# A two-branch sparse-attention decoder step: the prompt's compression units put into the first pair's products, and the samples' rows of W_out computed in column-tiled fp32 sets

## The chip, the cores and the metric

The kernel runs on one core of one Trainium2 chip, with one launch. The metric is device time in microseconds (us); the time before is the median of three runs. A profile of one execution comes beside it: what each engine did and when. The engines are PE (TensorE; PEld is its loading of weights, which overlaps the products), DVE (VectorE), ACT (ScalarE), POOL (GpSimd) and SP (SyncE, which here issues nearly all transfers). Lines such as L351 are lines of the kernel.

## The reference

One layer of a decoder, run for a prompt (512 tokens) and for 8 samples with one new token each and 1,024 cached tokens. Both share all weights. Cut to what matters here:

```python
shift, scale, gate = jnp.split(jax.nn.silu(c) @ w_ada + b_ada, 3, axis=-1)
h = x * (1.0 + scale[:, None, :]) + shift[:, None, :]
parts = jnp.split(h @ w_in, np.cumsum(IN_WIDTHS)[:-1], axis=-1)
...
def compress(kseq, pos_emb, w1, b1, w2, b2):      # blocks of 32 tokens, one every 16
    blk = kseq[:, idx] + pos_emb[None, None, :, None, :]
    blk = blk.transpose(0, 1, 3, 2, 4).reshape(bsz, n, g, CMP_LEN * dh)
    return jax.nn.gelu(blk @ w1 + b1) @ w2 + b2
...
y_a = (o_a * jax.nn.silu(a_z)) @ w_up_a
y_b = (o_b * jax.nn.silu(b_z)) @ w_up_b
mixed = (jax.nn.sigmoid(m_a) * y_a + jax.nn.sigmoid(m_b) * y_b) @ w_out
x_new = layer_norm(DEEPNORM_ALPHA * x + gate[:, None, :] * mixed, ln_g, ln_b)
```

`o_a` is native sparse attention (a compressed branch, a selected branch and a window), `o_b` is block-sparse attention. `compress` runs over the prompt's new keys and values, and over the cached ones of each sample. D_MODEL is 1,024, a head has 64 channels, and the compressed branch has two key/value heads.

## The kernel before

Activations lie transposed: channels on the 128 partitions, the 512 prompt tokens and 8 sample tokens along the free axis (NT = 520, worked in halves of HB = 260). Products of the heavy kind are made in three passes of a reduced fp32 format: a high part and the rest of each operand, as high x high, rest x high, high x rest. Splitting an operand costs an ACT cast (the high part) and a subtraction on DVE or POOL (`lo`, L362, recorded as L367). Which of the two subtracts is set by `LO_ENG`, three short patterns for three stages, cycled through.

*Order of the work.* Python generators with costs (`Flow`, `merge`) interleave several strands of work as they are written down. The order in which each engine then executes is written out by hand: `QUEUES` holds, for each of five engines, a list of numbers of its instructions, and `line_up` ties each to the one before it. `SLOTS` names, for each tile that rotates among buffers, which buffer each request takes.

*Start.* `ada` (L567) makes the adaLN vectors of 128 channels as fp32 products whose four members of a set write to 32 partitions each, on 32 columns of the array; `ada_h` (L575) makes the hidden tile h with its high part and rest; `early_mm` multiplies it with the weights of `kc`, `vc` and `ks` as soon as one tile of h is there. SP loads `cT`, the first constants and `bT` with three transfers (L640 to L643); x comes in eight rows (`load_x`, L544), four in tiles of the key/value pool and four in tiles of their own.

*Dense products.* `dense` (L690) makes 128 output channels in 48 products of 260 columns. Its weights come through a `Feed` (L408): a ring of four raw tiles of 128 x 1,024 (tag `wr`), each freed once its two halves are split into `hl`.

*Compression.* `units` (L926) takes 48 products: two (keys, values) times eight chunks of 256 channels times three passes. `phi_prompt` (L968) runs it for the prompt: 64 unit columns and 2 columns of position embedding, so products of 66 columns; from the last two columns comes the constant `cc`. Then `phi_pair` (L1013) runs it four times, each for a pair of samples, with 256 columns. `gelu` follows, and a second, small product (`second`). Both use the tile `u`, of which there are two buffers, one each for keys and values. The strand `phis` (L1145) runs beside the first dense products.

*The end.* `up` (L1631) makes the merged branch `m` for 128 channels, split; its 8 sample columns are copied, high part and rest, into `msh` (128 x 8 x 16). The output projection works in two halves of 512 output channels. The first half, `out_first` (L1800), goes along with `up`; the weights of the second half are loaded, split and kept by `load_second` (L1813) at the turns named in `SECOND`, and used at the end. Per tile of 128 prompt tokens `out_mm` takes 3 products for each of 8 channel tiles. The samples have products of their own, `out_samples` (L1708): for each of 8 channel tiles two products of 512 columns with 16 stationary columns, for both halves 32 in all. `samples` (L1713) adds their two parts with a small product (constant `selw`) and finishes their rows; `residual` and `norm` finish the prompt's.

Of the kernel before, what the change touches and what calls it, by code (L numbers as in the profile page):

```python
# [50 lines left out]
SECOND = [3, 4, 6, 7]  # L51
# [6 lines left out]
COPY_ENG = "daa"  # L58
NRAW, NHL, CRAW = 4, 3, 3
LO_ENG = "dp", "pd", "dp"  # L60
# [11 lines left out]
for _name, _w in (("ident", 128), ("seli", 10), ("rowmask", 1), ("ones", 1), ("p16", 1),  # L72
                  ("gsum", 128), ("oneb", 8), ("onem", 8), ("seln", 32), ("selx", 32),
                  ("selm", 4), ("w14", 14), ("w4", 4), ("maskn", 384), ("maskh", 128), ("maskm", 512),
                  ("selp", 128), ("sels", 32), ("selw", 32), ("selm4", 32)):
    _C[_name] = (_n, _n + _w)
    _n += _w
# [10 lines left out]
    "phi.u": "01010010101010",  # L88
    "ring.wr": "0133212023011031201301023120203102130321030123331202130231132102313021302",
    "kv.v2": "010101010",  # L90
    "kv.ev": "010101010101010011001100110011010101",
    "kv.kd": "012021021012012",
    "kv.kl": "01",
    "start.xr": "0123",
    "ps.s": "0101010101011010101010110100101101101011010010101001100010110011001101010101100110011001001110101100110101010101010101011001",
    "start.a": "01010101",
    "ps.d": "01210201201112002012102010202102120120110210210221012021021002201201200120201210210110210102120120012102102102101202102120220212102120221011"
        "20210",
    "ring.whl": "012012021021020120210120120120120120102102101202102012102102101202102101201201201020120120102012012012021210120",
    "phi.craw": "13200130120321302031",  # L100
# [3 lines left out]
    "at.q2": "0120120120120120",  # L104
    "at.qx": "0120120102102102",
    "at.mg": "01010101010101",
    "at.sm": "012345670123456701234567012354670123546701235467012354670123546701235467012354670123546701235467",
    "at.p3": "010101010101010101010101",
    "de.cr": "01200120120120120120120121202012012012012012",
# [12 lines left out]
    "fin.hs": "01",  # L122
# [6 lines left out]
0-1 5-8 2-3 20-23 9-12 24-27 4 13-17 34-35 18-19 36-41 31-33 28-30 42-55 58-63 56-57 67-69 95-97 64-66 92-94 70-77 89-91 81-83 123-125 86-88 84-85  # L129
78-80 120-122 98-105 109-111 151-153 114-116 106-108 148-150 112-113 126-133 117-119 140-141 145-147 176-178 137-139 142-144 134-136 162-164 154-161  # L130
170-172 165-169 179-181 207-209 182-189 204-206 222-224 196-197 193-195 173-175 201-203 198-200 190-192 210-212 225-227 231-233 219-221 213-215
228-230 216-218 246-251 234-239 252-257 240-245 258-263 270-275 264-269 276-281 310-312 282-285 313-318 335-338 319-321 286-289 322-324 290-297
325-330 342-344 298-301 345-356 302-305 357-359 306-309 360-362 390 363-365 339-341 331-334 366-389 415-419 403-408 391-396 409-414 397-402 420-425
444-447 432-437 467-475 426-431 476-481 491-493 482-484 438-443 494-496 515-520 466 497-505 485-490 506-508 454-459 509-511 521-526 448-453 460-465
527-538 512-514 539-544 551-562 545-550 563-574 587-592 602-616 575-586 632-634 656-673 617-622 635-637 623-628 638-643 629-631 644-655 680-685
674-679 692-697 686-691 698-703 749-757 704-709 716-721 758-760 710-715 761-763 593-595 764-766 773-775 596-598 776-781 722-733 767-769 782-784
797-802 770-772 599-601 785-787 734-739 803-808 821-826 788-793 827-832 794-796 833-844 857-862 809-820 863-868 845-856 869-880 890-907 914-916
908-910 917-922 911-913 740-742 926-931 923-925 950-955 932-934 944-949 935-937 743-748 962-967 938-943 956-961 968-979 1007-1012 986-991 980-985
1013-1018 992-997 881-889 1019-1042 1055-1060 1043-1048 998-1006 1049-1054 1097-1104 1061-1066 1079-1090 1129 1091-1096 1067-1072 1142 1105-1116
1167-1170 1073-1078 1117-1128 1136-1141 1183 1130-1135 1143-1154 1161-1166 1171-1176 1155-1160 1177-1182 1196 1184-1195 1203-1208 1215-1220 1197-1202  # L140
1282-1283 1209-1214 1268-1269 1231-1236 1227-1230 1221-1226 1237-1242 1244-1249 1298-1300 1243 1250-1255 1290-1291 1301-1305 1270-1275 1256-1267
1276-1281 1284-1289 1312-1313 1328-1329 1306-1311 1320-1321 1292-1297 1336-1339 1314-1319 1322-1327 1364-1365 1348-1351 1340-1345 1330-1335 1358-1359
1366-1373 1346-1347 1374-1375 1352-1357 1376-1395 1402-1407 1396-1399 1412-1417 1400-1401 1408-1411 1442-1447 1418-1421 1360-1363 1428-1431 1452-1459
1432-1433 1422-1427 1440-1441 1448-1451 1460-1467 1434-1439 1472-1479 1468-1471 1490-1495 1506-1507 1480-1485 1488-1489 1486-1487 1508-1513 1518-1523
# [199 lines left out]
def build(tc, A):  # L344
# [11 lines left out]
    def ld(out, x):  # L356
        return nc.sync.dma_start(out, x)  # L357

    D = {}
    turns, engs = [0], [LO_ENG[0]]  # L360

    def lo(out, x, hi, eng=None):  # L362

# [8 lines left out]
    with ExitStack() as es:  # L372
# [1487 lines left out]
        for k in range(8):  # L1860
            out_samples(p, k, keep[k])
# [134 lines left out]
```

## Time and profile before

| | us |
|---|---|
| median of 3 runs | 602.77 |
| the runs | 602.71, 602.77, 605.0 |
| the profiled execution | 605.51 |
| its span, first to last instruction | 603.8 |

The page has these parts: 1, busy time, share and instructions of each engine; 2, the span in 40 slices of about 15 us, with the clock that TensorE was granted (PEclk) and the DMA's load; 3, DMA queues; 4, the chain of work that ended last, by engine and by line; 5, the costliest groups of instructions, as line, engine, operation, out<-in, shapes, count | busy us, mean ns of one | idle us of the engine just before them, and what ended it; 6, DMA issues. Views that ask the trace further: groups that keep shapes apart, windows (busy time of each engine in a stretch), the timeline, the chain in order of time, and waits. Each timeline row has a start, a length, the engine, the line, out<-in, the shape, and in brackets the idle time before it. A product's recorded length overlaps with those of its neighbours.

### The profile page before, as it was taken

The numbers are of one execution on the slowest core, as the hardware profiler recorded it, in microseconds if no ns is written. First come the engines' busy times: TensorE is split into PE (matmuls) and PEld (weight loads), VectorE is DVE, ScalarE is ACT, GpSimd is POOL, SyncE is SP. The second block draws the span as 40 slices with busy tenths as digits, with TensorE's granted clock in tenths as the row PEclk, the third lists the DMA queues.
The fourth block names the chain that finished last, engine by engine and source line by source line (L and its number), as shares of the span: only waits on it lengthen the run. The fifth ranks groups of instructions, "written<-read, shape, count | busy, mean of one in ns | idle before, by whom it ended". The sixth has DMA issues, their size and how long they took to land.

```text
span 603.8 us, 13227 instructions
## 1 busy us (share of the span) xinstructions
PE 588.1 (97%) x4721; PEld 504.0 (83%) x4721; DVE 293.2 (49%) x824; ACT 291.3 (48%) x688; POOL 271.5 (45%) x317
## 2 busy tenths in 40 slices
PE   7999999999999999999999999999999999999994
PEld 4789999999997888878768899987878697989773
DVE  1556534334374664644363545676421245334187
ACT  2457565635546546634446454575534134233343
POOL 0222567563433724351446728346361455354406
PEclk9998899999999999999999999999999999999998
DMA  8995465811665574466968635822997996332403
GB/s 300 401 362 169 111 195 162 277 36 36 185 183 166 186 246 144 161 234 240 370 226 324 246 122 197 279 104 57 325 399 245 374 347 222 106 117 89 188 1 141
DMA packets 63955, 124.82 MB, mean 207 GB/s; under 512 B 8402, under 2 KB 26258, under 8 KB 63378
## 3 DMA queue, kind: packets, MB, share of 16 engines
q1 hardware_dynamic: 62482, 119.79, 58.6%
q0 software_dynamic: 1408, 4.20, 1.8%
q8 instruction: 37, 0.61, 0.4%
q14 instruction: 28, 0.23, 0.1%
HBM read 114.37 MB, written 9.58 MB: 205 GB/s over the span
## 4 chain that ended last, share of the span: by engine, by line
PE 79%; DVE 6%; DMA 5%; ACT 3%; POOL 2%; issue 2%; SPq 2%; POOLq 0%; ACTq 0%; DVEq 0%
PE d L351 47%; PE s L351 12%; PE e L351 7%; PE o L351 5%; PE pt L354 5%; PE pt L351 2%; SPq L357 2%; DMA raw<-w_cols 2%; DMA u<-ada_ss 1%; DMA raw<-ada_g 1%; DVE bn L1762 1%; DMA raw<-mobv 1%; POOL p L1243 1%; DVE xt L1758 1%; POOL u L367 1%
## 5 line engine op out<-in xcount | busy, mean ns | idle before, releaser
L351 PE MATMUL d<-hTh,hl 128*128 128x260 f32 (+1 forms) x1392 | 266.4, 288 | 0.7 <-POOL hl L367 0.5
L351 PEld LDWEIGHTS d<-hTh,hl 128*128 128x128 f32 (+1 forms) x1392 | 217.1, 189 | 5.0 <-issue 1.7
L351 PE MATMUL d<-hTl,hl 128*128 128x260 f32 (+1 forms) x704 | 199.7, 284 | 0.0
L351 PEld LDWEIGHTS d<-hTl,hl 128*128 128x128 f32 (+1 forms) x704 | 132.5, 188 | 0.0
L367 POOL TENSOR_TENSOR hl<-raw,hl 128x512 fp32r<-128x512 f32 x57 | 77.3, 1356 | 113.8 <-ACT hl L447 91.4
L447 ACT CAST hl<-raw 128x512 fp32r<-128x512 f32 (+1 forms) x111 | 68.0, 617 | 51.4 <-PE d L351 43.9
L1241 ACT ACTIVATE p<-s,sm 128x256 f32<-128x256 f32 (+3 forms) x96 | 50.6, 529 | 71.5 <-DVE sm L1238 47.7
L1243 POOL TENSOR_SCALAR p<-p,sm,gp 128x512 f32<-128x512 f32 (+3 forms) x64 | 42.4, 670 | 70.8 <-DVE sm L1242 57.9
L367 DVE TENSOR_TENSOR hl<-raw,hl 128x512 fp32r<-128x512 f32 (+1 forms) x54 | 43.0, 800 | 40.8 <-ACT hl L447 37.8
L351 PE MATMUL d<-yh,hl 128*128 128x260 f32 x256 | 47.2, 285 | 0.0
L351 PEld LDWEIGHTS d<-yh,hl 128*128 128x128 f32 x256 | 39.9, 188 | 3.1 <-issue 1.7
L354 PE MATMUL pt<-cst,p 128*128 128x128 f32 x240 | 39.9, 279 | 0.6 <-POOL p L1243 0.6
L1243 POOL TENSOR_SCALAR p<-p,sm,cst 128x128 f32<-128x128 f32 (+3 forms) x32 | 20.9, 661 | 38.6 <-ACT pp L1251 16.4
L354 PEld LDWEIGHTS pt<-cst,p 128*128 128x128 f32 x240 | 27.2, 141 | 12.8 <-POOL p L1243 3.0
L351 PE MATMUL d<-yl,hl 128*128 128x260 f32 x128 | 36.3, 283 | 0.0
L1251 ACT COPY pp<-pt 128x512 f32<-128x512 f32 (+1 forms) x48 | 22.9, 478 | 27.0 <-PE pt L354 26.4
L351 PE MATMUL s<-u,w1h 128*128 128x256 f32 (+1 forms) x160 | 35.0, 287 | 0.6 <-POOL u L367 0.3
L1236 DVE TENSOR_REDUCE sm<-s 128x1 f32<-128x128 f32 (+1 forms) x48 | 16.8, 354 | 37.1 <-PE s L351 30.7
L1238 DVE CUSTOM_DVE_ANT_0 s<-s,band 128x256 f32<-128x256 f32 (+1 forms) x48 | 17.3, 365 | 34.5 <-PE s L351 24.7
L351 PE MATMUL s<-kd,q 128*128 128x256 f32 (+3 forms) x96 | 33.0, 348 | 0.2 <-ACT p L1241 0.2
L351 PE MATMUL s<-kd,qx 128*128 128x256 f32 (+3 forms) x96 | 30.6, 322 | 0.0
L351 PEld LDWEIGHTS s<-u,w1h 128*128 128x128 f32 x160 | 28.2, 198 | 1.2 <-POOL u L367 0.5
(413 smaller groups left out, 1044.8 us busy)
## 6 DMA issues: line engine op xcount, KB each, us to landing
raw<-w_cols SPq DMA_DIRECT2D x46, 512.0 KB, 6.0
raw<-mobk SPq DMA_DIRECT2D x64, 256.0 KB, 4.5
raw<-mobv SPq DMA_DIRECT2D x64, 256.0 KB, 5.3
craw<-cmp SPq DMA_DIRECT2D x64, 128.0 KB, 2.8
u<-ada_ss SPq DMA_DIRECT2D x12, 512.0 KB
raw<-slck SPq DMA_DIRECT2D x64, 64.0 KB, 3.0
raw<-ada_g SPq DMA_DIRECT2D x8, 512.0 KB, 5.5
raw<-w_up SPq DMA_DIRECT2D x8, 512.0 KB
```

Source lines behind the costliest of these rows:

```text
L351: return mmraw(out, lhsT, rhs, start=start, stop=stop, skip_group_check=True)
L354: return nc.tensor.transpose(out, x, unit)
L357: return nc.sync.dma_start(out, x)
L367: (nc.gpsimd if eng == "p" else nc.vector).tensor_sub(out, x, f32(hi))
L447: nc.scalar.copy(h, src)
L1236: nc.vector.tensor_reduce(sm[:, 0:1], s[:, :b], axis=AX, op=OP.min)
L1238: nc.vector.tensor_tensor_reduce(out=s[:, b:n], in0=s[:, b:n], in1=j.band[:, 256 - (n - b):], scale=1.0, scalar=top, op0=OP.add, op1=OP.mi ...
L1241: nc.scalar.activation(pr, s[:, :n], AF.Exp, scale=-1.0, bias=sm[:, 1:2], accum_out=sm[:, 2:3])
L1243: D.setdefault("pool", []).append(nc.gpsimd.tensor_scalar(pr, pr, sm[:, 3:4], j.gate(i), op0=OP.mult, op1=OP.mult))
L1251: j.copied[gi] = (nc.scalar.copy if COPY_ENG[gi] == "a" else nc.vector.tensor_copy)(t[:, :n], p[:, :n])
L1758: nc.vector.tensor_add(xt[tt][:, c], xt[tt][:, c], p)
L1762: nc.vector.bn_stats(BN[tt][0][:, BN[tt][1]], xt[tt][:, c0 + k:c0 + min(k + 256, n)])
```

## The change

It does the following.

- The prompt's compression units join those of the first pair: `phi_pair(0)` gets `u` tiles of 16 x 161 x 2 columns (`PAIR` = 128 + 32 + 1; the last column of each half holds the position embedding), so its 48 products have 322 columns; the prompt's own 48 products of 66 columns, its own `gelu` and three products of its `second` are gone.
- `msh` holds the samples' columns of `m` in fp32, 128 x 8 x 32 with 24 zero columns. `out_samples` is called eight times (once in each `out_first`, once in each `load_second`) and makes four fp32 products of 256 columns from the raw weight tile of W_out, each on its own 32 columns of the array. They all add up in one PSUM tile. `selw` grows to pick rows out of four groups.
- `cT`, `bT` and the first constants are one tile and one transfer; x rows 4 to 7 use the tiles of rows 0 to 3; the first tile of h is made in two halves.
- `LO_ENG` gives way to two written lists, `HL_LO` (weights) and `LO` (the rest), with one letter for each subtraction.
- `SECOND` is [3, 5, 7, 8] in place of [3, 4, 6, 7], with the fourth load behind `out_first(6)`.
- `SLOTS` and all five lists of `QUEUES` are made anew.

```diff
-SECOND = [3, 4, 6, 7]
+SECOND = [3, 5, 7, 8]
...
+PAIR = 128 + 32 + 1
 NRAW, NHL, CRAW = 4, 3, 3
-LO_ENG = "dp", "pd", "dp"
+HL_LO = "dpdpdpdppdppdpddpdppdpdpdpdppdpdpdpdpdpdpdpdpdpdpdpdpdpdpdpdpdpdpdpdpdpdpdpdpdpdppddpdpdpdppdppddpdppddpdppddpd"
+LO = "dpdpdppdpdddppddppdddpddppdpddpddppddppdppddpdpdpdpdpdpdpddpdpdppddppddp"
...
-        def u_tile(dtype=F32R):
-            return pp.tile([128, 2, 2048], dtype, name="u", tag="u", bufs=2)
+        def u_tile(dtype=F32R, n=2048):
+            return pp.tile([128, 2, 16 * PAIR], dtype, name="u", tag="u", bufs=2)[:, :, :n]
...
-            D["act"] = nc.scalar.activation(hTh[:, j, :T], x[:, :T], AF.Identity, scale=s1[:, 0:1], bias=sh[:, 0:1])
+            if j:
+                D["act"] = nc.scalar.activation(hTh[:, j, :T], x[:, :T], AF.Identity, scale=s1[:, 0:1], bias=sh[:, 0:1])
+            else:
+                c = slice(0, HB)
+                nc.scalar.activation(hTh[:, j, c], x[:, c], AF.Identity, scale=s1[:, 0:1], bias=sh[:, 0:1])
+                nc.vector.tensor_scalar(h[:, c], x[:, c], s1[:, 0:1], sh[:, 0:1], op0=OP.mult, op1=OP.add)
+                nc.vector.tensor_sub(hTl[:, j, c], h[:, c], f32(hTh[:, j, c]))
+                c = slice(HB, T)
+                nc.scalar.activation(hTh[:, j, c], x[:, c], AF.Identity, scale=s1[:, 0:1], bias=sh[:, 0:1])
...
-        nc.sync.dma_start(cT, A["cT"])
+        nc.sync.dma_start(first_in, A["first"])
         load_ada(0)
-        nc.sync.dma_start(cst0, A["cst"][:, :NC0])
-        nc.sync.dma_start(bT, A["bT"])
...
-            us = [u_tile().rearrange("p x (k q u) -> p x q k u", k=16, q=16) for _ in range(2)]
+            n = 16 * (PAIR if bp == 0 else 128)
+            uv = [u_tile(n=n) for _ in range(2)]
+            us = [u.rearrange("p x (k c) -> p x k c", k=16)[:, :, :, :128].rearrange("p x k (q u) -> p x q k u", q=16) for u in uv]
+            if bp == 0:
+                yield from phi_prompt(*kcvc, uv)
...
-            nc.gpsimd.tensor_copy(msh[:, c, 0:8], f32(m[:, 0, T:]))
-            nc.gpsimd.tensor_copy(msh[:, c, 8:16], f32(m[:, 1, T:]))
+            nc.gpsimd.tensor_copy(msh[:, c, :NS], us[0][:, T:])
...
-        def out_samples(p, k, hl):
-            for x in range(2):
-                mm(p[:16], msh[:, k], hl[:, x], k == 0 and x == 0, k == 7 and x == 1)
+        def out_samples(half, i, raw):
+            c = half * 256
+            for k in range(2):
+                for x in range(2):
+                    mm(first[4][grp(2 * k + x), c:c + 256], msh[:, 2 * i + k], raw[:, k * 512 + x * 256:k * 512 + x * 256 + 256], i == 0 and half == 0, i == 3)
...
-                out_samples(first[4], i, hl)
+            out_samples(0, k // 2, W.raw[W.units[W.used][0]])
...
                 nc.scalar.copy(t[:, 0], src)
                 lo(t[:, 1], src, t[:, 0])
+            out_samples(1, i, raw)
...
         out_first(6)
-        halves = [fin.tile([16, 512], F32, name="hs", bufs=2) for _ in range(2)]
-        nc.scalar.copy(halves[0], first[4][:16])
+        load_second(3)
+        hs = fin.tile([128, 512], F32, name="hs")
+        nc.scalar.copy(hs, first[4])
...
-        p = p_d()
-        for k in range(8):
-            out_samples(p, k, keep[k])
-        nc.scalar.copy(halves[1], p[:16])
-        few = samples(halves)
+        few = samples(hs)
```

The parts of PE's new order that the prediction speaks of (numbers are places in the order in which the program is written; 3724 to 3731, 3852 to 3859, 3980 to 3987 and 4012 to 4019 are the samples' products):

```diff
+3694-3699 3682-3687 3709-3711 3706-3708 3728-3731 3705 3732-3737 3700-3702 3718-3720 3712-3714 3738-3749 3715-3717 3721-3723 3750-3755 3768-3773
...
+3756-3767 3774-3779 3852-3859 3780-3785 3792-3797 3834-3836 3786-3791 3798-3803 3828-3830 3804-3809 3837-3839 3831-3833 3849-3851 3840-3842 3816-3821
...
+3914-3919 3938-3943 3920-3925 4024-4026 3926-3931 4052-4054 3944-3955 3974-3976 3959-3961 3968-3970 3977-3987 4012-4019 4027-4029 4055-4060 3988-3990
```

More of the change, by code (lines that the diff above doesn't have):

```diff
@@ L133 @@
[L133 to L136, printed above, removed]
@@ L359, in build @@
     D = {}
-    turns, engs = [0], [LO_ENG[0]]
+    engs, hl_engs = iter(LO), iter(HL_LO)
     def lo(out, x, hi, eng=None):
         if eng is None:
-            eng = engs[0][turns[0] % len(engs[0])]
-            turns[0] += 1
+            eng = next(engs)
         (nc.gpsimd if eng == "p" else nc.vector).tensor_sub(out, x, f32(hi))
@@ L447, in split_to @@
                     nc.scalar.copy(h, src)
-                    lo(l, src, h)
+                    lo(l, src, h, next(hl_engs))
                     self.part[self.ns] = hl
@@ L589, in ada_h @@
             nc.vector.tensor_copy(hTh[:, j, T:], h[:, T:])
-            nc.vector.tensor_scalar(h[:, :T], x[:, :T], s1[:, 0:1], sh[:, 0:1], op0=OP.mult, op1=OP.add)
-            D["dve"] = nc.vector.tensor_sub(hTl[:, j], h, f32(hTh[:, j]))
+            c = slice(0 if j else HB, T)
+            nc.vector.tensor_scalar(h[:, c], x[:, c], s1[:, 0:1], sh[:, 0:1], op0=OP.mult, op1=OP.add)
+            c = slice(c.start, NT)
+            nc.vector.tensor_sub(hTl[:, j, c], h[:, c], f32(hTh[:, j, c]))
         def less_last(t, src, last):
@@ L947, in gelu @@
         def gelu(us, n):
-            bs = pp.tile([128, 257], F32, name="bsh")
+            bs = pp.tile([128, 2 * PAIR + 1], F32, name="bsh")
             nc.gpsimd.memset(bs[:, n:n + 1], 0.0)
@@ L982, in phi_prompt, with second_prompt @@
                         for l2 in range(2):
[L983 removed]
+                            cp(ut[OWN[l2], x, :, g, 128:160], v[OWN[g], :, :, l2])
             yield 3000
[L985 to L1000 removed]
+        def second_prompt(p, x2):
+            lo(ck2[:, 1, :], x2, ck2[:, 0, :], "d")
+            for g in range(2):
+                rows = slice(g * 32, g * 32 + 32)
+                nc.vector.scalar_tensor_tensor(cv2[rows, g], p[rows, 448:512], 0.5, b2v[rows], op0=OP.mult, op1=OP.add)
         craw, nraw = {}, [0]
@@ L1024, in phi_pair @@
                 yield 2600
-            before()
+            if before:
+                before()
             yield 300
-            uv = [u.rearrange("p x q k u -> p x (k q u)") for u in us]
-            gl = yield from units(256, lambda kv, x, l: uv[kv][:, x, l * 256:l * 256 + 256])
+            n //= 8
+            gl = yield from units(n, lambda kv, x, l: uv[kv][:, x, l * n:l * n + n])
+            width = 320 if bp == 0 else 256
             def second():
@@ L1145, in phis @@
         def phis():
-            second = yield from phi_prompt(*kcvc)
+            second = None
             for bp in range(4):
@@ L1619, in build @@
         yh, yl = [Y2[k][0] for k in range(8)], [Y2[k][1] for k in range(8)]
-        msh = fin.tile([128, 8, 16], F32R, name="msh")
-        nc.gpsimd.memset(f32(msh), 0.0)
+        msh = fin.tile([128, 8, 32], F32, name="msh")
+        nc.gpsimd.memset(msh, 0.0)
         cst3 = fin.tile([128, NC4 - NC3], F32, name="cst3")
```

311 lines of the change are left out of this document (151 added, 160 removed).

## The prediction

> **What bounds the kernel now.** I read the page first, its busy shares, its slices and its chain.
>
> ```profile
> span 603.8 us, 13227 instructions
> PE 588.1 (97%) x4721; PEld 504.0 (83%) x4721; DVE 293.2 (49%) x824; ACT 291.3 (48%) x688; POOL 271.5 (45%) x317
> PEclk9998899999999999999999999999999999999998
> PE 79%; DVE 6%; DMA 5%; ACT 3%; POOL 2%; issue 2%; SPq 2%; POOLq 0%; ACTq 0%; DVEq 0%
> ```
>
> PE has work in 97% of the span and no other engine in half of it, and the chain that ended last lies on PE for 79%. So a product taken away is worth its place in PE's queue, its pitch (the time from one product's end to the next one's), not its duration, because products overlap. From the chain and the timeline of PE, 260 and 256 columns first, then two forms that the change touches:
>
> ```profile
> 43.72 6.13 PE d L351 x51
> 94.32 2.88 PE s L351 x24
> 51.59 0.28 PE L351 MATMUL s<-u,w1h 128*128 128x66 f32 x1
> 51.70 0.28 PE L351 MATMUL s<-u,w1l 128*128 128x66 f32 x1
> 51.81 0.28 PE L351 MATMUL s<-u,w1h 128*128 128x66 f32 x1
> 572.99 1.55 PE L351 MATMUL e<-hl,msh 128*16 128x512 f32 x6
> L351 PE MATMUL e<-hl,msh 128*16 128x512 f32 x16 | 4.7, 395 | 0.4 <-DVE hl L367 0.4
> ```
>
> 51 products in 6.13 us and 24 in 2.88 us are 0.120 us each. A product of 66 columns follows the one before by 0.11 us: it saves nearly nothing by being a quarter as wide. For 512 columns, (1.55 - 0.395) / 5 = 0.231 us. Between 260 and 512 columns a column costs (231 - 120) / 252 = 0.44 ns.
>
> The slices show two eights in PEclk, so I cut the windows view there. Columns: window, its length, busy time of PE, PEld, DVE, ACT and POOL, granted clock, DMA share, GB/s.
>
> ```profile
> 50.00:56.80 6.80, 6.53 (x58) 6.42 (x58) 4.70 (x10) 6.31 (x12) 1.88 (x2) 1.00 0.61 186
> 56.80:63.60 6.80, 6.80 (x36) 6.80 (x36) 2.08 (x7) 1.91 (x5) 0.00 (x0) 0.50 0.20 60
> 63.60:70.00 6.40, 6.40 (x55) 6.17 (x55) 3.97 (x10) 5.18 (x13) 3.90 (x4) 1.00 0.20 63
> 59.87 0.40 PE L351 MATMUL s<-u,w1h 128*128 128x66 f32 x1
> 60.08 0.40 PE L351 MATMUL s<-u,w1l 128*128 128x66 f32 x1
> ```
>
> For 6.8 us the clock is halved: 36 products where the next 6.4 us hold 55, and 66 columns at a pitch of 0.21 us. That loses 6.8 / 2 = 3.4 us. It comes right after the stretch in which the 66-column products stand close together, the thinnest work between the head and the tail. The Trainium skill, in "TensorE: Matmul & The Clock Gate", section "What's actually happening", says that the array's clock is halved after a window of about 3.4 us of low activity and given back by activity; the clock of 0.50 behind the thin stretch agrees, though no run yet shows the cause.
>
> **The change part by part.** *Compression.* What goes are these products, and what stays wider is the third group:
>
> ```profile
> L351 PE MATMUL s<-u,w1h 128*128 128x66 f32 x32 | 7.7, 292 | 0.3 <-ACT u L983 0.3
> L351 PE MATMUL s<-u,w1l 128*128 128x66 f32 x16 | 4.9, 308 | 0.0
> L351 PE MATMUL s<-u,w1h 128*128 128x256 f32 x128 | 27.3, 286 | 0.4 <-POOL u L367 0.3
> 107.32 0.28 PE L351 MATMUL pt<-w2l,gl 128*128 128x64 f32 x1
> 107.43 0.28 PE L351 MATMUL pt<-w2h,gl 128*128 128x64 f32 x1
> ```
>
> 48 products at 0.11 us go: 5.3 us. The first pair's 48 grow from 256 to 322 columns: 48 x 66 x 0.44 ns = 1.4 us more. In the second product three of 64 columns go (3 x 0.11 = 0.3 us), three grow by 64 columns (0.1 us). Net -4.1 us at full clock. The prompt's own gelu chain goes too, and the copies of its units stay; both lie on ACT, DVE and POOL, about half idle. The first pair's products now wait for the prompt's copies and the cache chunks; before, the chunks' copies waited for the prompt's products, 4.29 us:
>
> ```profile
> 60.73 0.62 ACT L1022 CAST u<-craw 128x512 fp32r<-128x512 f32 x1 [4.29 <-PE s L351]
> ```
>
> That wait goes, and dense products (5.8 us for 48) have to fill PE meanwhile. I put this at nothing; without that cover it costs up to the same 4.3 us.
>
> *The clock.* With the 66-column products gone, the stretch of 50 to 57 us fills with products of 260 columns, as around it. I take -3.4 us, ends 0 and -3.4.
>
> *Samples.* 32 products of 512 columns at 0.231 us go: 7.4 us. In their place stand 32 fp32 products of 256 columns, in eight sets of four, each member on 32 columns of the array. The nearest row is the adaLN product, of the same form and width, 8 products recorded twice each, two sets:
>
> ```profile
> 17.30 0.28 PE L351 MATMUL d<-hTl,v 128*128 128x260 f32 x1
> 17.51 1.07 PE L351 MATMUL s<-u,cs 128*32 128x256 f32 x16
> 18.51 0.30 PEld L351 LDWEIGHTS d<-hTh,v 128*128 128x128 f32 x2 [0.41 <-issue]
> 18.51 0.51 PE L351 MATMUL d<-hTh,v 128*128 128x260 f32 x2
> ```
>
> The product before ends at 17.58 us and the sets at 18.58: 0.50 us a set. The next two products end 0.44 us later in place of 2 x 0.12: going back to the full array costs 0.2 us. PE's new order puts six sets in three pairs (3852-3859, 3977-3987, 4012-4019), one right behind the gate's spread, which is in this form already (3648-3651 3724-3727), and one alone, so four new returns: 8 x 0.50 + 4 x 0.2 = 4.8 us, and -2.6 us. Ends: no return felt, -3.4; all eight felt at the weight loader's whole 0.41 us, 4.0 + 3.3 = 7.3, so -0.1.
>
> *Head.* One transfer replaces three, kc's weights are issued fifth instead of twelfth, and the first h tile is made in halves.
>
> ```profile
> 0.00:5.00 5.00, 2.07 (x4) 1.17 (x4) 0.23 (x1) 1.54 (x2) 0.76 (x6) 1.00 0.53 178
> 5.00:15.00 10.00, 8.86 (x57) 5.08 (x57) 2.12 (x10) 2.35 (x5) 0.00 (x0) 1.00 0.99 361
> 9.16 5.44 DMA raw<-w_cols
> 13.47 0.81 ACT L586 ACTIVATE hTh<-ev,ssh 128x512 fp32r<-128x512 f32 x1
> 14.86 0.59 PE L351 MATMUL d<-hTh,kd 128*128 128x260 f32 x2
> 19.68 2.27 SPq L550 DMA_DIRECT2D xr<-xT x3
> ```
>
> DMA is at 0.99 of its time from 5 us on. Before, kc's weights landed last, at 9.16 + 5.44 = 14.6 us; now the first x row stands behind them, so the bytes ahead of the first dense products are about the same. What is won is half of the 0.81 us activation and some order: -0.8 us, ends 0 (x lands last) and -2.0 (PE's first dense product at 13 us instead of 14.86). Rows 4 to 7 of x now reuse the tiles of rows 0 to 3 and must wait for them to be read; they were issued from 19.68 us, after row 0's use at 13.47, so nothing.
>
> *All else*: eight fewer small copies on POOL, other turns for DVE and POOL, other loads of W_out's second half, new orders. Their sign can't be read from an order. PE's waits on named engines are short (below), so 0, with ends of -3 and +4. The tail behind PE's last product stays.
>
> Sum: -4.1 - 3.4 - 2.6 - 0.8 = -10.9 us. The profiled execution took 605.5 us, so 594.6. The median of the three runs, 602.8, is 2.7 us below it, near the price of the slow stretch; I can't see whether those runs had it. From the median: 602.8 - 10.9 = 591.9 if they did, 602.8 - 7.5 = 595.3 if not. I say 594.0.
>
> **The rivals.** *The clock stays*, or halves elsewhere, for instance where PE now waits for the first pair. For it: the narrow gate products (64 columns of the array) remain in that stretch, and PE has thinner work there. Against: the thin products go. Price 3.4 us: 597.4, with the bounds of the rest 596 to 600.
>
> *Each set empties the array twice.* "TensorEngine Tiling (Array Packing)", section "Key Properties", in the Trainium skill, states that changing the tiling mode drains TensorE; the weight loader's 0.41 us agrees. By rows: if each of the eight paid 0.41 us on the way in and out, 8 x (0.50 + 0.82) = 10.6 us replace 7.4, +3.2 instead of -2.6: 599.8. Against: the row shows no gap on the way in, and three pairs are shared.
>
> *Gaps eat it.* New orders or the longer first pair leave PE idle for 8 us: about 602. These are what PE's products and its weight loader waited for between 70 and 560 us (total, times, longest):
>
> ```profile
> PE d L351 <- POOL hl L367: 0.5, 1, 0.5
> PEld pt L354 <- POOL p L1243: 3.0, 5, 0.8
> ```
>
> There is little now, so it would have to be new.
>
> *Slower: raw weights hold the ring.* A set reads the raw tile, which before was free once ACT and DVE or POOL had split it; now it is also held until PE reaches the set. The four slots are loaded in order by SP, so a load that waits for a slot holds up all others behind it, and PE waits for w_up.
>
> ```profile
> raw<-w_cols SPq DMA_DIRECT2D x46, 512.0 KB, 6.0
> L447 ACT CAST hl<-raw 128x512 fp32r<-128x512 f32 (+1 forms) x111 | 68.0, 617 | 51.4 <-PE d L351 43.9
> L367 POOL TENSOR_TENSOR hl<-raw,hl 128x512 fp32r<-128x512 f32 x57 | 77.3, 1356 | 113.8 <-ACT hl L447 91.4
> 500.00:560.00 60.00, 59.64 (x408) 51.89 (x407) 24.37 (x47) 19.36 (x34) 30.27 (x36) 1.00 0.42 135
> ```
>
> A load needs 6.0 + 0.6 + 1.4 = 8 us before PE can use it; three loads ahead of 5.8 us each are 17 us. A hold under 9 us costs nothing, beyond it each us is one of PE. To end slower by over 0.5% (3 us), eight holds have to give back 10.9 + 3 = 14 us, 1.7 us each beyond the nine: 606. DMA at 135 GB/s in that stretch speaks against it.
>
> **How the numbers follow.** Forecast 0.60, clock stays 0.20, sets drain twice 0.07, gaps 0.07, ring 0.06. The range is 587 to 600: down to the sum's best ends (head -2.0, samples -3.4, orders -3, from the median), up over the kept clock and most of the draining sets; it leaves out gaps and ring. A measurement of this kernel tells about 0.5%, 3 us, from no change: faster is below 599.8. Forecast, clock and half of the draining sets are faster, 0.84; the rest of those and the gaps are the same, 0.10; the ring is slower, 0.06.
>
> **What would show it.** Right: no group of 66 columns, 48 products of 322; PEclk 1.00 from 50 to 64 us; no 128*16 products, and each pair of sets taking 1.0 us with about 0.2 us before the next; first dense product near 14 us; PE's busy time down by about 11 us. Wrong: a clock of 0.50 anywhere before the tail, weight loads waiting for DMA raw or for DVE and POOL after 500 us, or gaps on PE before the first product of 322 columns.

## The result and the profile after

The kernel with the change takes 607.47 us (median; 606.35 to 608.08), the kernel before beside it 603.32 us (602.71 to 605.0): a ratio of 1.006, 95% interval 1.0041 to 1.0079, or +3.6 us (2.5 to 4.8). The forecast was 594.0 us, in a range of 587 to 600; the change is slower, and the time lies outside the range.

The profiled execution took 607.65 us. Its page, by the lines that the prediction showed of before:

```profile
span 605.9 us, 13138 instructions
PE 583.6 (96%) x4702; PEld 499.6 (82%) x4702; DVE 302.7 (50%) x824; ACT 290.0 (48%) x685; POOL 266.6 (44%) x304
PEclk9999999999999999999999999999999999999997
PE 63%; DVE 6%; ACT 3%; DMA 2%; issue 1%; POOL 1%; SPq 1%; POOLq 0%; ACTq 0%; DVEq 0%
```

PE is busy for 4.5 us less (588.1 before) and the span is 2.1 us longer (603.8), so PE sits idle 6.6 us more. The chain lies on PE for 63%, where it was 79%. PE's products are now the ones that the forecast had, but its busy time was to fall by about 11 us. Groups and timeline rows of after:

```profile
L353 PE MATMUL s<-u,w1h 128*128 128x322 f32 x32 | 7.6, 315 | 0.0
L353 PE MATMUL s<-u,w1l 128*128 128x322 f32 x16 | 5.0, 310 | 0.0
L353 PE MATMUL e<-raw,msh 128*32 128x256 f32 x64 | 4.3, 384 | 0.0
16.39 0.59 PE L353 MATMUL d<-hTh,v 128*128 128x260 f32 x2
563.47 1.93 PE L353 MATMUL e<-raw,msh 128*32 128x256 f32 x32
565.34 2.35 PE L353 MATMUL d<-big,m 128*128 128x512 f32 x9
```

No group of 66 columns is left, and none of 128*16. Four sets take 1.93 us, 0.48 us each (0.50 was forecast), and the nine products behind them end 2.29 us after them, in place of 9 x 0.231 = 2.08: 0.2 us for the return, as forecast. The eight sets stand in four places, one of them right behind the gate's spread, so three returns are new and not four. But the first dense product stands at 16.39 us (14.86 before; 14 was forecast), and there are gaps. PE's waits in after, longest first (total, times, longest; before had 2.2 us for `cs` and the same 1.1 us for `zn`):

```profile
PE s L353 <- DVE cs L658: 3.3, 1, 3.3
PE d L353 <- DVE ev L790: 2.6, 1, 2.6
PE pt L356 <- DVE pp L1264: 1.1, 1, 1.1
PE e L353 <- POOL zn L650: 1.1, 1, 1.1
PE d L353 <- DVE m L368: 1.0, 1, 1.0
PE e L353 <- DVE pr L1096: 0.9, 1, 0.9
```

The stretch that the prediction cut out, in after (columns as there):

```profile
50.00:56.80 6.80, 5.56 (x47) 5.32 (x45) 4.64 (x6) 4.28 (x9) 4.43 (x3) 1.00 0.34 133
56.80:63.60 6.80, 5.48 (x33) 5.48 (x34) 5.18 (x12) 6.19 (x13) 1.34 (x2) 0.75 0.69 196
63.60:70.00 6.40, 6.40 (x56) 6.21 (x55) 4.44 (x8) 4.31 (x11) 3.73 (x4) 1.00 0.76 243
```

Before, PE was busy for 13.3 of the first 13.6 us. Now it is busy for 11.0, and half of the second window still runs at half clock. From PE's last product to the end it is 8.5 us before (595.2 to 603.75) and 10.3 us after (595.5 to 605.9). So the gain reached PE's queue and was lost again. The sum had -10.9 us, and between the two profiled executions it is +2.1: 13.0 us apart. The head has 2.3 of them (1.5 lost and 0.8 not won), the wait at 55 to 58 us 2.6, the three new gaps of about 1 us (`pp`, `m`, `pr`) 3.0, the tail 1.8, and the half clock that stayed 1.7, together 11.4.

### The profile page after: what moved, and what is told of

It reads as the page before. It is cut to its first block, busy times and chain, and to the rows that moved or that the text cites. A ratio compares the mean times of both kernels' runs of the same rounds, so it can differ in the third digit from the quotient of the medians.

```text
span 605.9 us, 13138 instructions
## 1 busy us (share of the span) xinstructions
PE 583.6 (96%) x4702; PEld 499.6 (82%) x4702; DVE 302.7 (50%) x824; ACT 290.0 (48%) x685; POOL 266.6 (44%) x304
## 4 chain that ended last, share of the span: by engine, by line
PE 63%; DVE 6%; ACT 3%; DMA 2%; issue 1%; POOL 1%; SPq 1%; POOLq 0%; ACTq 0%; DVEq 0%
PE d L353 37%; PE e L353 8%; PE s L353 7%; PE o L353 6%; PE pt L356 5%; DMA xt<-xn 1%; PE pt L353 1%; DMA raw<-w_cols 1%; DVE bn L1774 1%; ACT xt L1696 1%; DVE xt L1770 1%; ACT p L1254 1%; DVE d L1769 0%; PE d L356 0%; PE e L356 0%
## 5 line engine op out<-in xcount | busy, mean ns | idle before, releaser
L368 POOL TENSOR_TENSOR hl<-raw,hl 128x512 fp32r<-128x512 f32 x57 | 74.7, 1310 | 119.8 <-ACT hl L448 107.6
L1254 ACT ACTIVATE p<-s,sm 128x384 f32<-128x384 f32 (+3 forms) x96 | 50.6, 529 | 58.6 <-DVE sm L1251 44.1
L1256 POOL TENSOR_SCALAR p<-p,sm,gp 128x256 f32<-128x256 f32 (+3 forms) x64 | 41.0, 648 | 72.5 <-DVE sm L1255 65.5
L368 DVE TENSOR_TENSOR hl<-raw,hl 128x512 fp32r<-128x512 f32 (+1 forms) x54 | 46.4, 860 | 28.6 <-ACT hl L448 28.4
L356 PE MATMUL pt<-first_in,p 128*128 128x128 f32 x240 | 39.9, 279 | 1.6 <-DVE pp L1264 1.1
L356 PEld LDWEIGHTS pt<-first_in,p 128*128 128x128 f32 x240 | 27.2, 141 | 13.7 <-ACT p L1254 2.5
L1256 POOL TENSOR_SCALAR p<-p,sm,first_in 128x128 f32<-128x128 f32 (+3 forms) x32 | 22.7, 715 | 24.1 <-DVE sm L1255 21.5
L353 PE MATMUL o<-pp,v 128*64 128x512 f32 (+3 forms) x192 | 29.7, 441 | 0.0
L353 PE MATMUL s<-u,w1h 128*128 128x256 f32 (+1 forms) x128 | 29.5, 294 | 0.0
```

Of the source, the lines that this page charges most:

```text
L353: return mmraw(out, lhsT, rhs, start=start, stop=stop, skip_group_check=True)
L356: return nc.tensor.transpose(out, x, unit)
L368: (nc.gpsimd if eng == "p" else nc.vector).tensor_sub(out, x, f32(hi))
L1254: nc.scalar.activation(pr, s[:, :n], AF.Exp, scale=-1.0, bias=sm[:, 1:2], accum_out=sm[:, 2:3])
L1256: D.setdefault("pool", []).append(nc.gpsimd.tensor_scalar(pr, pr, sm[:, 3:4], j.gate(i), op0=OP.mult, op1=OP.mult))
```

## The experiments

Two theories stood at the start. *Orders*: the removed products are worth their pitch, and the new hand-written orders put waits in their place that can be mended. *Next wait*: in the places that the change touches, something else is ready only shortly before PE, so that a product taken out uncovers it, in whatever order. All ratios are to the kernel before on the same chip.

### The start's transfer ahead of the two halves of the first weights (after)

```diff
 "SP":
-1 5 0
+0-1 5
```

> The changed kernel with one move in SyncE's order: the transfer of first_in is issued ahead of the two ada halves instead of behind them. Theory (the change's savings are real and the new orders gave them back, the head 1.6 us of them): adaLN's first product starts near 6 us instead of 8.23, the first dense product about 1.5 us sooner than 16.39, and the time falls by about 1.6 us against the changed kernel, to near 606 us. Rival (the head's delay is absorbed later, or the wait moves on to the ada halves themselves): the time falls by less than 0.5 us.

607.37 us, ratio 1.0066 (1.0037 to 1.0094), as without the edit. The wait for `cs` was gone, and PE waited for the next thing instead:

```profile
PE s L353 <- DMA u<-ada_ss: 3.4, 4, 1.3
```

The adaLN's first product came 3.1 us sooner (5.09 us in place of 8.23), the first dense product only 0.4 us (15.98 in place of 16.39): ScalarE's first step on x now waited for x's own transfer until 14.4 us, with the DMA at 0.87 of its time in the first 15 us (0.85 in after). This execution, with 613.3 us the slowest of its kernel, also ran at half clock from 11.3 to 18.1 us, so what the head gives at full clock can't be read from it. By the time, the rival held.

### The gates' steps sooner on VectorE (after)

```diff
 "DVE":
-70 68-69 67 64 79 81 74 78 57 73 76 80
+64 70 79 68-69 67 81 80 74 78 57 73 76
```

> The changed kernel with one move in VectorE's order: the second subtraction of kd and the gates' two adds stand ahead of the prompt's four copies of 2.64 us instead of behind them. Theory (orders gave the savings back): the idle 2.55 us of TensorE at 55.6 us goes, and the granted clock, which falls to half for 3.4 us from 58.4 us, stays whole, worth about 1.7 us; together 3 to 4.6 us off the changed kernel. Rival (the stall only moves: the four copies are late next, at the products that need u): the time falls by less than 1 us and a wait for u of about 2 us appears between 55 and 70 us.

607.36 us, ratio 1.0077 (1.0049 to 1.0104). The time is the rival's. Its wait for `u` didn't come; the one wait of 2.6 us became two others:

```profile
PE d L353 <- DVE v L758: 1.6, 1, 1.6
PE d L353 <- ACT ev L728: 1.6, 1, 1.6
```

They end at 58.2 and 65.0 us, and in this execution the clock stayed whole there. Mending this order moved the stall, it didn't remove it.

### The tail in the order of before (after)

```diff
 "Activation":
-556 558 555 552
+558 552 556 555
```

The last 20 places of VectorE's list go back to before's order as well.

> The changed kernel with VectorE's last twenty places in the order of the kernel before (the last residual ahead of the samples' scaling and of the last norm but one), and with ScalarE's casts of the second half's weights ahead of the activations on xt. Theory (orders gave the savings back): the time between TensorE's last product and the end goes from 10.3 us back to near 8.5 us, and the wait of 0.96 us at 575.5 us goes: about 2.5 us off the changed kernel. Rival (the end is set by the transfers out, not by VectorE's order): less than 0.6 us off, and the tail stays over 10 us.

606.98 us, ratio 1.0066 (1.0039 to 1.0093). In the profile PE's last product ended 2.6 us sooner than in after, at 592.9, and yet it took 10.5 us from there to the end. VectorE is the reason. Two rows of before and three of this kernel, VectorE and then GpSimd:

```profile
592.61 0.51 DVE L1739 TENSOR_SCALAR xs<-xs,smv 128x256 f32<-128x256 f32 x1
591.68 1.28 POOL L1794 TENSOR_TENSOR xt<-xt,ln 128x512 f32<-128x512 f32 x1
```

```profile
591.83 1.42 DVE L1752 TENSOR_SCALAR xs<-xs,smv 128x256 f32<-128x256 f32 x1
595.67 0.42 DVE L1770 TENSOR_TENSOR d<-d,gb 128x256 f32<-128x256 f32 x1
590.57 2.53 POOL L1807 TENSOR_TENSOR xt<-xt,ln 128x512 f32<-128x512 f32 x2
```

VectorE has no gap from 588 to 597 us, and one of its steps takes 1.42 us in place of 0.51. GpSimd was at work in before too: the step ends 0.16 us behind GpSimd's instruction there (592.96 and 593.12 us) and 0.15 us behind it here (593.10 and 593.25). What differs is how much of GpSimd's instruction was left when it started. The last residual starts at 595.67 us, as before (595.53), whenever PE is done. The end follows VectorE and GpSimd.

### All three at once (after)

> The changed kernel with the three moves of the other runs together: first_in sooner, the gates ahead of the prompt's copies, the last twenty places of VectorE as before with the casts sooner. Theory (orders gave the savings back, in places that do not touch each other): the sums add, 7 to 8 us off the changed kernel, to about 600 us, 0.5 per cent below the kernel before. Rival (the savings were never there, each repaired wait is followed by the next one): within 2 us of the changed kernel.

606.96 us, ratio 1.0059 (1.0031 to 1.0086). The three mended orders together are worth nothing that can be measured, where 7 to 8 us were expected: *orders*, as I had it, fell.

### The samples' part alone, in before's orders

```diff
-                mm(p[:16], msh[:, k], hl[:, x], k == 0 and x == 0, k == 7 and x == 1)
+                    mm(first[4][grp(2 * k + x), c:c + 256], msh[:, 2 * i + k], raw[:, k * 512 + x * 256:k * 512 + x * 256 + 256], i == 0 and half == 0, i == 3)
```

> The kernel before with only the samples' part of the change: eight column-tiled sets in place of the 32 narrow products, every queue otherwise in the order of the kernel before. Theory (a part is worth its PE time as long as the order around it stays): -2.6 us, ratio 0.9957. Rival (TensorE's work is not what ends the time in these places, whatever the order): within 1 us of the kernel before, because VectorE's chain sets the last 15 us.

609.16 us, ratio 1.0104 (1.0062 to 1.0146): +6.3 us (3.7 to 8.8) where -2.6 was forecast; the rival, within 1 us, failed as well. Waits that before doesn't have, and then two windows:

```profile
PE pt L353 <- DVE xt L1761: 2.4, 1, 2.4
PE s L353 <- DMA raw<-ada_g: 1.5, 1, 1.5
```

```profile
489.00:493.50 4.50, 3.72 (x17) 2.06 (x18) 1.85 (x2) 0.23 (x1) 3.44 (x5) 0.62 1.02 401
578.00:582.00 4.00, 3.57 (x16) 2.41 (x17) 3.57 (x10) 0.78 (x3) 0.00 (x0) 0.57 0.01 4
```

Between 564 and 576 us before had all 16 products of the samples' second half and six of the first, and VectorE came to its four residuals behind them. Without them PE comes to the samples' small product 2.4 us before VectorE frees its accumulator. At 490 us the wait is for a load, with the DMA at 1.02 of its time. Behind both the clock halves, for 3.4 us each: the granted 0.62 and 0.57. From the first product of the adaLN's gate (`s<-raw,cs`, at 445.4 us in before and 444.1 here) to PE's last product, this kernel takes 153.6 us and before 149.8, 3.8 us more. The two waits (3.9 us) and the half clock (twice 1.7 us) cost 7.3, so the products by themselves are about 3.5 us cheaper, near the 2.6 of the forecast.

### The compression part alone, in before's orders

```diff
+PAIR = 128 + 32 + 1
...
-                        o = u[:, :n + 2] if n == 64 else u[:, :n]
-                        mm(o, wa[:, kv, l, :], r, l == 0 and j == 0, l == 7 and j == 2)
+                        mm(u[:, :n], wa[:, kv, l, :], r, l == 0 and j == 0, l == 7 and j == 2)
```

> The kernel before with only the compression part of the change (the prompt's units as columns 256 to 321 of the first pair's products; rows 4 to 7 of x reuse the tiles of rows 0 to 3, which the space needs), every queue otherwise in the order of the kernel before. Theory (a part is worth its PE time as long as the order around it stays): -4.1 us, ratio 0.993. Rival (TensorE's work is not what ends the time here): within 1.5 us of the kernel before, with TensorE waiting for the first pair's casts instead.

607.2 us, ratio 1.0057 (1.0034 to 1.008): +3.4 us (2.1 to 4.8) where -4.1 was forecast; the rival's time, within 1.5 us, failed as well, though a wait came. Its longest waits behind the head, and then its window of 47 to 57 us beside before's:

```profile
PE d L353 <- DVE ev L784: 2.7, 1, 2.7
PE s L353 <- DVE x L953: 1.4, 1, 1.4
```

```profile
47.00:57.00 10.00, 7.91 (x67) 7.64 (x66) 8.25 (x17) 9.70 (x19) 2.06 (x3) 0.99 0.58 172
```

```profile
47.00:57.00 10.00, 9.73 (x85) 9.54 (x84) 7.59 (x16) 9.14 (x18) 1.88 (x2) 0.99 0.61 181
576.00:590.00 14.00, 14.00 (x77) 10.74 (x75) 12.17 (x33) 6.77 (x14) 1.29 (x1) 1.00 0.01 1
```

In before, ScalarE is busy for 9.14 of these 10 us and VectorE for 7.59: the prompt's casts into `u`, the split of `kd`, the gates' copies. The thin products had filled PE's time up to the end of that. The last row, also of before, has VectorE at 12.17 of 14 us.

From PE's first dense product to the first product of the attention (`s<-kd,q`; 14.86 and 165.45 us in before, 15.78 and 165.90 here) the two programs have the same products but for this part. It takes 150.6 us in before and 150.1 us here, with 6.8 us of half clock in each. So in its own stage the part is worth 0.5 us.

### Both parts, in before's orders

> Both parts together, every queue otherwise in the order of the kernel before. Theory (the orders made anew gave the savings back): the parts add, -6.7 us, ratio 0.989, near 597 us. Rival (the parts never had that worth): the ratio lies within 0.4 per cent of 1, as the changed kernel's does.

610.21 us, ratio 1.0106 (1.0068 to 1.0145): +6.4 us (4.1 to 8.7). That is outside both expectations. In the orders made anew it is +3.6 (2.5 to 4.8); the intervals overlap, so the new orders are no worse than before's and not shown to be better.

### The thin products out, and nothing in their place

```diff
+                        if n == 64 and (l or j):
+                            continue
-                        mm(o, wa[:, kv, l, :], r, l == 0 and j == 0, l == 7 and j == 2)
+                        mm(o, wa[:, kv, l, :], r, l == 0 and j == 0, n == 64 or l == 7 and j == 2)
```

> The kernel before with 46 of the 48 products of 66 columns left out (the prompt's compressed keys and values are then not computed), all orders as before: what their TensorE time is worth by itself. Theory (TensorE's work there ends last): -5 us, ratio 0.992. Rival (something else ends last there, and the thin products stand in its shadow): less than 1.5 us.

602.24 us, ratio 0.9978 (0.9953 to 1.0003): -1.3 us (-2.8 to +0.2) for 5.1 us of PE work. The new wait:

```profile
PE s L354 <- ACT u L988: 2.4, 1, 2.4
```

*Next wait* held: even at no price for what replaces them, these products were worth about a quarter of their pitch, and the interval includes no gain at all. In the stage from the first dense product to `s<-kd,q` the profiled execution takes 145.1 us (15.71 to 160.76) with the clock whole, before 150.6 us, or 147.2 without the 3.4 us of its half clock: 2.1 us saved.

### The thin products twice

```diff
-                        mm(o, wa[:, kv, l, :], r, l == 0 and j == 0, l == 7 and j == 2)
+                        for again in range(2 if n == 64 else 1):
+                            mm(o, wa[:, kv, l, :], r, l == 0 and j == 0 and not again,
+                               l == 7 and j == 2 and again == (n == 64))
```

> The kernel before with each of the 48 products of 66 columns of the prompt's compression run twice, the second right behind the first, all else in its place (the prompt's compressed keys and values come out of doubled sums). It adds 48 x 0.11 us = 5.3 us of TensorE work at 41 to 62 us, where leaving 46 of them out was worth 1.3 us. Theory (TensorE is the last to be ready in these places, with something else 1 to 3 us behind it, so that work taken out is paid only down to that next wait): what is added is paid in full, +4 to +5.3 us, ratio 1.007 to 1.009. Rival (the stage's time is not what sets the end at all, later waits for transfers and VectorE give or take what an early stage gains): under +2.5 us, ratio below 1.004.

613.91 us, ratio 1.014 (1.0087 to 1.0193): +8.5 us (5.3 to 11.7) for 5.3 us of PE work. What is added is paid at least in full. The clock has a share in it: the profiled execution has 10.2 us of half clock from 62.4 us on, where before had 6.8.

### The samples' products twice

```diff
-                mm(p[:16], msh[:, k], hl[:, x], k == 0 and x == 0, k == 7 and x == 1)
+                for again in range(2):
+                    mm(p[:16], msh[:, k], hl[:, x], k == 0 and x == 0 and not again, k == 7 and x == 1 and again == 1)
```

> The kernel before with each of the 32 products of the samples' part of W_out run twice (the samples' rows come out of doubled sums). It adds 32 x 0.231 us = 7.4 us of TensorE work at 511 to 576 us. Theory (TensorE last, the next wait close behind): +6 to +7.4 us, ratio 1.010 to 1.012. Rival (the end is set by VectorE's and GpSimd's chain of the last layer norm, with room ahead of it): under +4 us, ratio below 1.0065.

610.66 us, ratio 1.0105 (1.0076 to 1.0134): +6.3 us (4.6 to 8.1) for 7.4 us of PE work.

### The samples' products out

```diff
+                if k or x:
+                    continue
-                mm(p[:16], msh[:, k], hl[:, x], k == 0 and x == 0, k == 7 and x == 1)
+                mm(p[:16], msh[:, k], hl[:, x], True, True)
```

> The kernel before with 30 of the 32 products of the samples' part of W_out left out (the samples' rows come out of a part of their sum), all else in its place. It takes 30 x 0.231 us = 6.9 us off TensorE at 511 to 576 us. Prediction's way of counting (each removed product is worth its pitch): -6.9 us, ratio 0.989. Theory (the next wait close behind): -1 to -3 us, with a new wait of TensorE for VectorE near 576 us or a longer tail, ratio 0.995 to 0.998.

601.64 us, ratio 0.9952 (0.9922 to 0.9982): -2.9 us (-4.7 to -1.1) for 6.9 us of PE work, with the wait of the kernel above that has the samples' sets alone:

```profile
PE pt L354 <- DVE xt L1763: 2.4, 1, 2.4
```

In the profile PE's last product ends 4.4 us sooner than before (590.8 against 595.2), with the same 6.8 us of half clock at 56.8 us in both, and the tail is 0.5 us longer. So PE kept 4.4 of the 6.9 us, and the wait took the rest.

### Both out

The two edits above that leave products out, together.

> The kernel before with 46 of the 48 products of the prompt's compression and 30 of the 32 products of the samples' part of W_out left out, nothing put in their place (the prompt's compressed keys and values and the samples' rows come out of parts of their sums). It takes 5.1 + 6.9 = 12.0 us of TensorE work away, all that both parts of the change could take. Theory (each place pays only down to the next wait): the two results singly added, -1.3 - 2.9 = -4.2 us, ratio 0.993. Prediction's way of counting: -12.0 us, ratio 0.980.

599.59 us, ratio 0.9937 (0.9907 to 0.9967): -3.8 us (-5.6 to -2.0). That is close to the sum of the two (-4.2) and a third of the 12.0 us of work. The waits of the profiled execution, the slowest of this kernel (606.14 us):

```profile
PE s L353 <- ACT u L987: 2.4, 1, 2.4
PE pt L353 <- DVE xt L1764: 2.4, 1, 2.4
```

### The samples' return later (samples' part alone)

```diff
 "PE":
-4071-4074 4064 4155-4157 4109-4117 4158-4160
+4064 4155-4157 4109-4117 4158-4160 4071-4074
```

> The kernel with the samples' sets alone in the orders of before (1.010 times before), with the four products that bring the samples' sums back moved 16 products later in TensorE's queue, so that the 2.4 us wait for VectorE near 576 us and the 3.4 us of half clock behind it have no cause there. If that wait is where the gain went: TensorE's last product 3 to 4 us sooner, and the time 3 to 4 us below that kernel's, ratio to before 1.003 to 1.005. If the end there is set by VectorE's chain and not by TensorE: the last product sooner but the time within 1 us of that kernel's, ratio 1.008 to 1.012.

609.55 us, ratio 1.0086 (1.005 to 1.0121), against 1.0104. The wait of 2.4 us is gone, and two others came behind it, for the samples' layer norm on VectorE:

```profile
PE pt L353 <- DVE smv L1729: 1.3, 1, 1.3
PE pt L353 <- DVE smv L1736: 1.3, 1, 1.3
```

The ratio lies in the rival's range, but the interval reaches both expectations, and in the profiled execution the head lost about 3 us to half clock (6.8 us from 12.1 us on), so that the end of PE's last product (599.4 us) can't be set beside the other kernel's.

### Three casts to GpSimd (compression part alone)

```diff
-                            cp(ut[OWN[l2], x, :, g, 128:160], v[OWN[g], :, :, l2])
+                            f = nc.gpsimd.tensor_copy if kv and not x and (g or not l2) else cp
+                            f(ut[OWN[l2], x, :, g, 128:160], v[OWN[g], :, :, l2])
```

> The kernel with the compression part alone in the orders of before (1.0057 times before), with three of ScalarE's casts of the prompt's keys and values into u (together 1.92 us at 53.4 to 55.3 us) moved to GpSimd, which is idle there for 3.4 us. Theory (in that stage ScalarE's casts end last, at 57 us, and the thin products of before had only filled the time up to there): TensorE's wait of 2.7 us for the gates' copy ev near 55 us shrinks by 1.5 us or more, and the time by 1.5 to 2.5 us, ratio 1.0015 to 1.0035. Rival (VectorE's and GpSimd's own queues end as late): the wait stays above 2 us or stands again at a later place of the same pair, ratio 1.0045 to 1.007.

608.06 us, ratio 1.009 (1.0053 to 1.0127), against 1.0057. Not only is the wait still there, it grew from 2.7 to 3.8 us. Timeline rows of VectorE, ScalarE and GpSimd:

```profile
53.03 1.13 DVE L368 TENSOR_TENSOR kd<-ev,kd 64x512 fp32r<-64x512 f32 x1
54.88 0.51 DVE L975 TENSOR_TENSOR u<-pos,u 128x16 fp32r<-128x16 f32 x1
56.49 0.69 DVE L368 TENSOR_TENSOR kd<-ev,kd 64x512 fp32r<-64x512 f32 x1
57.34 0.36 ACT L782 COPY ev<-d 24x260 f32<-24x260 f32 x1 [2.99 <-DVE kd L368]
52.93 2.41 POOL L985 CAST u<-eh 64x256 fp32r<-64x256 f32 x3
```

ScalarE is done early and waits 3.0 us for VectorE's second subtraction of `kd`, and VectorE is late because its steps stretch while GpSimd casts: 1.13 us where the same step behind it takes 0.69. My theory, that ScalarE's casts end last, fell: VectorE ends as late.

### The gates ahead of the casts (compression part alone)

```diff
 "Activation":
-50 48 51 36 58 28 54
+36 50 48 54 51 58 28
 "DVE":
-73 69 74 71 62 77
+62 73 69 77 74 71
```

> The kernel with the compression part alone in the orders of before (1.0057 times before), where on ScalarE and on VectorE the second half of kd and the gates' copy ev go ahead of the last casts of the prompt's keys and values into u, nothing else moved. Theory (near 55 us TensorE waits for VectorE's queue, not for ScalarE's: with ScalarE freed the wait grew from 2.7 to 3.8 us): the wait for ev shrinks to about 1 us and the time by 1.5 us or more, ratio 1.002 to 1.0035. Rival (the casts put behind are the next thing that TensorE waits for, or the time comes from elsewhere): TensorE's remaining work at 65 us and the time as in that kernel, ratio 1.0045 to 1.007.

606.68 us, ratio 1.0048 (1.0025 to 1.0071), against 1.0057. With both queues cleared, the gates' copy found the next thing, the tile's outgoing transfer (the execution runs 3 us later here, from the head on):

```profile
59.65 0.36 ACT L783 COPY ev<-d 24x260 f32<-24x260 f32 x1 [1.18 <-DMA ok<-ev]
60.52 0.63 PE L353 MATMUL d<-hTh,hl 128*128 128x260 f32 x2 [2.42 <-DVE ev L784]
```

So three things end close together there: ScalarE's casts, VectorE's subtractions, and the transfer that frees the buffer of `ev`. Clearing the first two moved PE's wait from 2.7 to 2.4 us.

## Why the prediction was wrong

| PE work, in the orders of before | forecast's way of counting, us | measured, us |
|---|---|---|
| thin products out | -5.1 | -1.3 (-2.8 to +0.2) |
| samples' products out | -6.9 | -2.9 (-4.7 to -1.1) |
| both out | -12.0 | -3.8 (-5.6 to -2.0) |
| thin products twice | +5.3 | +8.5 (5.3 to 11.7) |
| samples' products twice | +7.4 | +6.3 (4.6 to 8.1) |

**The step that failed** is the first one: "PE has work in 97% of the span", so "a product taken away is worth its place in PE's queue". The table shows that this holds for work added and not for work taken out. Taken out, it is paid only down to the next wait. In the profiled executions, at equal clock, 5.1 us less work saved PE 2.1 us and 6.9 us less saved it 4.4, with a new wait of 2.4 us in each; of the whole time it was 1.3 and 2.9 us, with more lost to the clock (below). The 97% could not tell: it is 97% with both sets of thin products in, 97% with either out, and 96% with both out. Nor could "PE's waits on named engines are short": a short wait says that PE came last, not by how much.

**Compression**, -4.1. Sized right on PE (48 products of 322 columns, recorded at 310 to 315 ns where 256 columns take 281 to 286), wrong in time. In its own stage it saved PE 0.5 us of the 4.1: the two new waits, 2.7 us for the gates' copy and 1.4 us for `x`, took the rest, since the pair's products now stand where ScalarE and VectorE are still at the prompt's copies. I wrote that these copies "lie on ACT, DVE and POOL, about half idle". That is the average of the span; my own row for 50.00 to 56.80 us had ScalarE busy for 6.31 of 6.80 us, and I read only the clock from it. Both attempts to take the first wait away moved it. They explain why nothing was won and not the whole +3.4 us. In the profiled executions 0.9 us more lie in the head and 0.8 us between 445 and 490 us, and the kernel's twelve executions lose 4.2 us (median) to the clock, where before beside it lost 2.4; how these share the 3.4 us stays open.

**The clock**, -3.4. There was little to win. Each execution has its mean granted clock, and (1 - clock) x time is what it lost by it. In 121 executions of the kernel before, two thirds lost 3.0 us or less, of which 2.1 us in the profiled one lie behind PE's last product, where they cost nothing. The 6.8 us of half clock at 56.8 us, worth 3.4, were in the profiled execution (605.5 us) and not in most of those that make the median of 603. I had seen the 2.7 us between the two and left it open. The sign was wrong too for products taken out: the median loss is 4.2 us without the thin products, 5.7 us without the samples' and 6.6 us without both, with the new gaps ahead of it, and 2.4, 2.4 and 3.0 us in before beside them. That is 1.8 to 3.6 us more, of the 3.8, 4.0 and 8.2 us of removed work that were not paid. (The tails of these three are within about 0.5 us of before's in the profiled executions, so little of it lies behind PE's last product.) In after the six executions lost 5.1 us (median); 0.9 us of that can be half of the 1.8 us by which its tail is longer.

The forecast's reason, the thin products, is not the whole matter. With them in once and in before's orders, the profiled execution has the halving near 57 us in two kernels (before, samples out) and not in three (samples' part alone, its return later, samples twice); with the thin products twice it lasts 10.2 us. Without them it stands near 57 us as well, behind a wait of 2.4 to 2.7 us, in after, in the compression part alone and in both out, though not in the thin products out alone. So taking the thin work away and putting a gap there could not be counted on to keep the clock.

**Samples**, -2.6. The eight sets take 3.9 us in after, 0.48 us each on average, and 0.2 us for each of three new returns, 4.5 us where 4.8 were forecast: the price of what was added is right. The Trainium skill, in "TensorEngine Tiling (Array Packing)", section "Key Properties", says that a change of tiling mode drains the array; the 0.2 us agree, and they are not the rival's 0.82 us for each set. The removed side was worth 2.9 us and not 7.4, so the part by itself should cost about 2 us. In before's orders it cost 6.3, with 3.9 us of waits and two stretches of half clock on top (3.4 us). Why the load at 490 us, ahead of the first set, comes late there isn't shown.

**Head**, -0.8: +1.5 us of a later first dense product. The joined transfer stood behind the first two halves of the adaLN weights, and PE waited 3.3 us for what is made from it. Putting it first changed what PE waits for and not the time; the rows of x and the first weights share a DMA at 0.85 of its time.

**All else**, 0 with ends -3 and +4. The gaps of about 1 us for `pp`, `m` and `pr` and the tail's 1.8 us are in that term. "The tail behind PE's last product stays" failed: VectorE paces it, and it was already at 12.17 of 14 us at 576 to 590 us.

**The rivals.** "Gaps eat it", with a chance of 0.07 and 602 us, is what happened, 5 us worse. "Clock stays" came true beside it. The ring, the only way to slower that I priced, has no wait in after; in the samples' part alone a wait of 1.5 us for a load stands at 490 us, before the first set.

What stays open: whether some other order would give the 4 us that both removals are worth and pay less for the replacements. Five mended orders were tried (and three of them together), and none gave time that can be measured.

## What to carry to other kernels

A busy engine at 97% says roughly what added work costs, not what removed work gives: for a removal, find in its own window how far behind the second engine, the transfers and the buffers are, and take the gain as the smaller of the two. The cheapest experiment on a removal comes before the rewrite: leave the work out with nothing in its place, and see what the best case is. A stretch of half clock in one profiled execution is a gain only if the other executions have it too.

## What the runs showed of the hardware

Up to PE's last product, the granted clock halves in stretches of 3.41, 6.83 and 10.24 us that start at 8 to 12, 56 to 62, 490 to 496 and 575 to 583 us and differ from kernel to kernel. The loss differs from execution to execution, too: 1.8 to 7.9 us over the 121 executions of the kernel before, and time follows it with 0.88 us per us (correlation 0.74). In the 3.41 us ahead of a halving PE was busy for 0.1 to 1.9 us in 21 of 25 cases and for 2.7 in one; in the other three (before, samples out, thin products twice) it was busy for 3.1 to 3.4 us, with the thin products. The Trainium skill, in "TensorE: Matmul & The Clock Gate", section "What's actually happening", has an activity window of about 3.4 us that runs freely and isn't tied to the kernel's start; the multiples agree, and it would make the halving fall differently each time.

Some of VectorE's steps stretch while GpSimd works: 0.51 to 1.42 us for one of the samples' layer norm, which ends 0.15 us behind GpSimd's instruction, and 0.69 to 1.13 us for a subtraction beside casts on GpSimd. Others keep their length. In "SBUF — State Buffer", section "SBUF: two separate sides", the Trainium skill describes a port pair shared by the two that one of them holds for a whole instruction; the row that ends with GpSimd's agrees. Three casts moved from ScalarE to GpSimd, idle there, went in that run with longer steps on VectorE and a longer wait of PE (3.8 us in place of 2.7). In after VectorE is busy for 302.7 us with 824 instructions, in before for 293.2 us with as many; how much of that comes from GpSimd isn't shown.
